# A gated recurrent and pooling layer: work tiles without zero columns in front, and all slots of 4,096 bytes

## The chip, the cores and the metric

The kernel runs on one core of one Trainium2 chip. The metric is the device time of one execution in microseconds. Engines are named as in the profile: PE is TensorE (matmuls), DVE is VectorE, ACT is ScalarE, POOL is GpSimd, SP is SyncE, which issues most DMAs.

## What is computed

One layer on x, 1,024 steps by 1,024 features, in float32 (reference, cut):

```python
h = x @ w_in + b_in                     # 1024 x 6144
xa, za, xb, zb, ga, gb = split(h)       # six of 1024
xa = causal_depthwise_conv(xa, conv_w, conv_b)          # 4 taps: y[t] = sum_k w[k] * x[t - 3 + k] + b
ya = rg_lru(xa, ...) * silu(za)         # gates by 64 x 64 head matrices, then h[t] = a[t] * h[t-1] + u[t]
yb = multiscale_pool(xb, ...) * silu(zb)
merged = sigmoid(ga) * (ya @ w_proj_a) + sigmoid(gb) * (yb @ w_proj_b)
x = layer_norm(alpha * x + merged @ w_out + b_out)

# the pool: feature group g of four has the window win = 2, 4, 8 or 16
cs = cumsum(xb, over time)
mean[t] = (cs[t] - cs[t - win]) / min(t + 1, win)
y = ((mean - xb) @ w_pool[g] + b_pool) * scale
```

So in front of the first step both the convolution and the window sums see zeros, and the first win - 1 columns of a pool are divided by their own count.

## The kernel before

Everything stands transposed: 128 features on the partitions and the 1,024 steps (S) along a row; H is 512, a half. Each product is done in float32r as three passes (high times high, high times low, low times high), and the 2 x 2 blocks of the large products are combined in seven products instead of eight. So most operands exist as a pair of tiles, high and low, made by a cast on ACT and a subtraction on DVE (`split`).

The first product is done group by group, 24 groups: G (two blocks of gates ga or gb), A (a block of xa and one of za) and B (a block of xb and one of zb), c being the block's number. While PE is at the next groups, DVE and ACT finish a group: for A the convolution (`a_front`), the head products `ps_g`, and the recurrence (`a_gates`); for B the window sums and the mean (`b_front`), then, for each pair of blocks, the product `ps_pool` with w_pool (`b_pool`). After the groups come the two merge products (tiles pa_, pc_, pe_) and the output product (oa, oc, oe) with the norm.

The program is first recorded as a list of tasks. A planner (`Plan.order`) then goes through them with costs of its own (`Plan.cost`) and due times, gives each engine its order, and emits everything from line 388; so the profile shows line 388 everywhere, and instructions are told apart by tile names. Each engine works through its own order strictly.

Tiles of 128 rows lie in pools: x (28 slots), w (10), r (4), k (10), e and g, in this order behind the constants. x, w and r slots have 4,096 bytes in each partition. A k slot is as large as the largest k tile. Which tiles are k tiles matters here: the front's working tiles xp, xc, xbp and the sums, xch and xcl (moving side of ps_g), mixh and mixl (moving side of ps_pool), and the pairs o1, o6, o7, o5, o3 and o4 (stationary side of oa and oc). The operands of the groups and of the merge products are x and w tiles throughout; the product oe has its operands in x and w tiles as well.

xp has three zero columns in front of the 1,024, xbp and the sums have PAD = 16, so that a shifted view reads zeros there. With 1,040 columns a k slot therefore takes 4,160 bytes. Where the slots start in a partition, as the built program lays them out (bytes):

| pool | before: first slot, step | start modulo 512 | after: first slot, step | start modulo 512 |
|---|---|---|---|---|
| x | 4,256, 4,096 | 160 | 4,320, 4,096 | 224 |
| w | 118,944, 4,096 | 160 | 119,008, 4,096 | 224 |
| r | 159,904, 4,096 | 160 | 159,968, 4,096 | 224 |
| k | 176,288, 4,160 | 160, 224, 288, 352, 416, 480, 32, 96, 160, 224 | 176,352, 4,096 | 224 |
| e | 217,888, 2,048 | 288 | 217,312, 2,048 | 224 |
| g | 226,080, 512 | 288 | 225,504, 512 | 224 |

Of the kernel before, what the change touches and what calls it, by code (L numbers as in the profile page):

```python
# [11 lines left out]
F32 = mybir.dt.float32  # L12
F32R = mybir.dt.float32r
AF = mybir.ActivationFunctionType
ALU = mybir.AluOpType

P = 128
S = 1024
D = 1024
NK = D // P  # L20
H = 512
# [4 lines left out]
PAD = 16  # L26
# [17 lines left out]
C_BIN = 0  # L44
C_CONVB = 48
C_CONVW = 56
# [354 lines left out]
def layer_kernel(ctx: ExitStack, tc: tile.TileContext, xq, x, w_in, par, wg, w_pool, wpa, wpb, w_out, rows, out):  # L401
    nc = Plan(tc)

    def pool(name, bufs, space=None):
        kw = {} if space is None else {"space": space}
        return Pool(ctx.enter_context(tc.tile_pool(name=name, bufs=bufs, **kw)), bufs, space is bass.MemoryType.DRAM)

    const = pool("const", 1)
# [3 lines left out]
    kpool = pool("kpool", NWORK)  # L412
# [11 lines left out]
    def rt(name, dt=F32, shape=(P, 2, H)):  # L424
        return rpool.tile(list(shape), dt, tag="r", name=name)

    def kt(name, dt=F32, w=S):
        return kpool.tile([P, w], dt, tag="k", name=name)

    def et(name):  # L430
        return epool.tile([P, H], F32, tag="e", name=name)
# [1 line left out]
    def bank(name):  # L433
        return psum.tile([P, H], F32, tag="ps", name=name)
# [5 lines left out]
    HALF = [slice(0, H), slice(H, S)]  # L440
    V, A = nc.vector, nc.scalar
# [4 lines left out]
    def pcol(base, c):  # L446
        return par_sb[:, base + c:base + c + 1]


    def split(raw, hi, lo):  # L450
        A.copy(hi, raw)
        V.tensor_tensor(lo, raw, hi.bitcast(F32), ALU.subtract)
# [141 lines left out]
    XA, ZA, XB, ZB, GA, GB = (8 * i for i in range(6))  # L594
# [13 lines left out]
    def weights_steps(i):  # L608
        kind, c = order[i]
        n1, n2 = blocks_of(kind, c)  # L610
        return Weights(f"{kind}{c}", w_in[n1], w_in[n2])
# [25 lines left out]
    def both(t, m1):  # L637
        for sl in HALF:
            V.tensor_tensor(t[:, sl], t[:, sl], m1, ALU.add)
# [83 lines left out]
    src = {}  # L723

    def a_outputs(c):
        xp, zt = kt(f"xp{c}", w=S + 3), kt(f"z{c}")
        V.memset(xp[:, 0:3], 0.0)

        def c11(ps, m1):
            V.scalar_tensor_tensor(xp[:, 3:3 + H], ps, pcol(C_BIN + XA, c), m1, ALU.add, ALU.add)  # L730

        def c12(ps, rest=None):
            if rest is None:
                A.activation(xp[:, 3 + H:], ps, AF.Identity, bias=pcol(C_BIN + XA, c))
            else:
                V.scalar_tensor_tensor(xp[:, 3 + H:], ps, pcol(C_BIN + XA, c), rest, ALU.add, ALU.add)

        def c21(ps, u2):
            V.tensor_tensor(zt[:, HALF[0]], ps, u2, ALU.add)

        def c22(ps, m7):
            V.tensor_tensor(zt[:, HALF[1]], ps, m7, ALU.add)

        def c2(m1):
            both(zt, m1)

        return (xp, zt), (c11, c12, c21, c22, c2)

    def a_front(c, xp, zt):
        xc = kt(f"xc{c}")  # L750
        V.tensor_scalar(xc, xp[:, 0:S], pcol(C_CONVW, 4 * c), pcol(C_CONVB, c), ALU.mult, ALU.add)
        for j in range(1, 4):
            V.scalar_tensor_tensor(xc, xp[:, j:j + S], pcol(C_CONVW, 4 * c + j), xc, ALU.mult, ALU.add)
        xh, xl = kt(f"xch{c}", F32R), kt(f"xcl{c}", F32R)
        split(xc, xh, xl)
        A.activation(zt, zt, AF.Silu, bias=pcol(C_BIN + ZA, c), scale=-1.0)
        return xc, xh, xl
# [80 lines left out]
        return finish, (c11, c12, c21, c22, c2)  # L838


    rcnt = const.tile([P, PAD], F32, name="rcnt")
    for t in range(PAD):
        nc.gpsimd.memset(rcnt[:, t:t + 1], 1.0 / (t + 1))
    mixed = [None] * NK
    szb = [None] * NK

    def b_outputs(c):
        xp, zt = kt(f"xbp{c}", w=S + PAD), kt(f"zb{c}")
        V.memset(xp[:, 0:PAD], 0.0)

        def c11(ps, m1):
            V.scalar_tensor_tensor(xp[:, PAD:PAD + H], ps, pcol(C_BIN + XB, c), m1, ALU.add, ALU.add)

        def c12(ps, rest=None):
            if rest is None:
                A.activation(xp[:, PAD + H:], ps, AF.Identity, bias=pcol(C_BIN + XB, c))
            else:
                V.scalar_tensor_tensor(xp[:, PAD + H:], ps, pcol(C_BIN + XB, c), rest, ALU.add, ALU.add)

        def c21(ps, u2):  # L860
            V.tensor_tensor(zt[:, HALF[0]], ps, u2, ALU.add)

        def c22(ps, m7):
            V.tensor_tensor(zt[:, HALF[1]], ps, m7, ALU.add)

        def c2(m1):
            both(zt, m1)

        return (xp, zt), (c11, c12, c21, c22, c2)

    def b_front(c, xp, zt):

        win = WINDOWS[c // 2]
        cur, step, lo = xp, 1, 0
        n = 0
        while step < win:
            nxt = kt(f"sum{n}_{c}", w=S + PAD)
            lo += step
            V.tensor_tensor(nxt[:, lo:], cur[:, lo:], cur[:, lo - step:S + PAD - step], ALU.add)
            cur, step, n = nxt, step * 2, n + 1  # L880
            yield
        m = cur[:, PAD:]
        e = win - 1
        V.tensor_tensor(m[:, 0:e], m[:, 0:e], rcnt[:, 0:e], ALU.mult)
        V.tensor_tensor(m[:, 0:e], m[:, 0:e], xp[:, PAD:PAD + e], ALU.subtract)
        V.scalar_tensor_tensor(m[:, e:], m[:, e:], 1.0 / win, xp[:, PAD + e:], ALU.mult, ALU.subtract)
        yield
        mh, ml = kt(f"mixh{c}", F32R), kt(f"mixl{c}", F32R)
        split(m, mh, ml)
        mixed[c] = (mh, ml)  # L890
        A.activation(zt, zt, AF.Silu, bias=pcol(C_BIN + ZB, c), scale=-1.0)
        szb[c] = zt
# [11 lines left out]
    def b_pool(g):  # L904
# [15 lines left out]
        if g == 1:  # L920
# [5 lines left out]
    sp, m, nl, y, z, z2, acc = (const.tile([P, 8], F32, name=n)  # L926
                                for n in ("sp", "sp_m", "sp_nl", "sp_y", "sp_z", "sp_z2", "sp_acc"))
# [23 lines left out]

    begin = ctx.enter_context(ExitStack())
    pass
    warm = kt("warm", F32R, H)
    V.memset(warm.bitcast(F32), 0.0)
    psw = bank("ps_warm")
    for i in range(WARM):
# [141 lines left out]
    w = weights_steps(1)  # L1099
# [19 lines left out]

    outs = g_outputs(GA, 0)[0]  # L1120
    tiles0, takes0 = a_outputs(0)
    g = Group("A0", w.out, X, *takes0)
    f5 = bank("f_A0")
# [23 lines left out]
    def first_rest(g=g):  # L1147
        g.m6()
        g.take(1, f5, g.u2)
        g.take(3, g.a, t5)  # L1150
        yield
        g.m4()
        yield
# [13 lines left out]
    for i in range(1, len(order)):  # L1167
        kind, c = order[i]
# [8 lines left out]
        if i == 1:  # L1177
            tiles = tiles0
        elif kind == "A":
            tiles, takes = a_outputs(c)  # L1180
        elif kind == "B":
            tiles, takes = b_outputs(c)
        else:
            finish, takes = g_outputs(GA if c < 4 else GB, c % 4)
# [20 lines left out]
        else:  # L1205
            g.m1()
            g.m2()
            if i == 2:
                rest = first_rest()
# [13 lines left out]
        if kind == "A":  # L1223
            def prev_end(c=c, tiles=tiles, i=i):
                front = a_front(c, *tiles)
                due.setdefault(i + 2, []).append(lambda: a_gates(c, *front, tiles[1]))
        elif kind == "B":
            def prev_end(c=c, tiles=tiles, i=i):
                for _ in b_front(c, *tiles):
                    pass  # L1230
                if c % 2 == 1:
                    pools.setdefault(i + 2, []).append(lambda: b_pool(c // 2))
        else:
            prev_end = finish
# [113 lines left out]
    def fronts():  # L1348
        for e in ends:
            yield from b_front(*e)  # L1350
# [6 lines left out]
    for i, (n, j) in enumerate(steps):  # L1357
# [7 lines left out]
        if j == 1:  # L1365
            a, c, m1, um = [[None] * KQ for _ in range(4)]
        X_, W_ = ([(hi_[:, k, :], lo_[:, k, :]) for hi_, lo_ in ops[i][o:o + 2] for k in range(2)] for o in (0, 2))
        for g in range(KQ):
# [4 lines left out]
            ps = a[g] if j in (1, 6, 5, 3) else c[g] if j != 2 else bank(f"pe_{n}{g}")  # L1373
# [31 lines left out]
            if (n, j, g) in CASTS:  # L1405
                k = CASTS.index((n, j, g))
# [12 lines left out]
    zt = {}  # L1419
# [76 lines left out]
    a, c = ([None] * KQ for _ in range(2))  # L1496
    operands(6)
    for i, j in enumerate(O_STEPS[:5]):
# [4 lines left out]
        for g in range(KQ):  # L1503
# [4 lines left out]
            ps = c[g] if j == 7 else a[g]  # L1508
# [13 lines left out]
    for g in range(KQ):  # L1522
# [3 lines left out]
        for sl in pieces:  # L1526
            ps = bank(f"oe_{g}_{sl.start}")[:, 0:sl.stop - sl.start]
# [58 lines left out]
```

## Time and profile before

| | |
|---|---|
| timed runs, us | 742.62, 743.99, 745.5; the median 743.99 |
| profiled execution | span 741.3 us from the first to the last instruction; the runs lie 1.3 to 4.2 us above it |
| mean granted TensorE clock | 0.998 |
| PE busy | 732.1 us, 99% |
| DVE busy | 599.6 us, 81% |
| ACT busy | 459.0 us, 62% |
| POOL busy | 68.2 us, 9% |
| traffic with main memory | 289 GB/s over the span |

The profile is one execution, with a page of sums and views of single stretches. In lists of instructions a row has the start, the length, the engine, the line, the operation, the tiles (out<-in, buffer numbers left out) and the shapes. A row of the chain that ended last has start, length, engine and output tile, with the number of instructions merged. A row of waits reads "who <- for whom: total, times, longest". A matmul's own length (389 ns) overlaps the next one's; how close they follow each other is seen from starts, or from a piece of the chain divided by its number of instructions.

### The profile page before, as it was taken

The numbers are of one execution on the slowest core, as the hardware profiler recorded it, in microseconds if no ns is written. First come the engines' busy times: TensorE is split into PE (matmuls) and PEld (weight loads), VectorE is DVE, ScalarE is ACT, GpSimd is POOL, SyncE is SP. The second block draws the span as 40 slices with busy tenths as digits, with TensorE's granted clock in tenths as the row PEclk, the third lists the DMA queues.
The fourth block names the chain that finished last, engine by engine and source line by source line (L and its number), as shares of the span: only waits on it lengthen the run. The fifth ranks groups of instructions, "written<-read, shape, count | busy, mean of one in ns | idle before, by whom it ended". The sixth has DMA issues, their size and how long they took to land.

```text
span 741.3 us, 8792 instructions
## 1 busy us (share of the span) xinstructions
PE 732.1 (99%) x3249; PEld 599.0 (81%) x3249; DVE 599.6 (81%) x749; ACT 459.0 (62%) x587; POOL 68.2 (9%) x118
## 2 busy tenths in 40 slices
PE   8999999999999999999999999999999999999996
PEld 6887887888788878888888888888888888888885
DVE  7999796959696878977986767879948886999676
ACT  7686959686877868688844445446543555324473
POOL 0071011111101111100011000100000000000021
PEclk9999999999999999999999999999999999999999
DMA  8237988588988989842187944998679996758657
GB/s 328 96 137 194 273 190 259 139 243 217 307 166 214 321 214 281 213 115 99 45 200 155 213 113 157 277 336 319 229 248 298 317 330 230 261 206 233 179 88 139
DMA packets 64227, 158.98 MB, mean 214 GB/s; under 512 B 4340, under 2 KB 8308, under 8 KB 64120
## 3 DMA queue, kind: packets, MB, share of 16 engines
q1 hardware_dynamic: 43512, 106.26, 41.3%
q0 software_dynamic: 20112, 51.91, 33.6%
q8 instruction: 25, 0.41, 0.2%
q10 hardware_dynamic: 560, 0.26, 0.1%
q14 instruction: 18, 0.15, 0.1%
HBM read 137.43 MB, written 77.07 MB: 289 GB/s over the span
## 4 chain that ended last, share of the span: by engine, by line
PE 98%; DMA 1%; DVE 1%; DVEq 0%; issue 0%
PE a_A L388 11%; PE a_B L388 11%; PE a_G L388 11%; PE oa L388 6%; PE pa_a L388 6%; PE pa_b L388 6%; PE c_B L388 6%; PE c_A L388 6%; PE c_G L388 5%; PE ps_pool L388 3%; PE oc L388 3%; PE pc_b L388 3%; PE pc_a L388 3%; PE e_B L388 3%; PE e_A L388 3%; PE ps_s L388 3%
## 5 line engine op out<-in xcount | busy, mean ns | idle before, releaser
L388 ACT ACT_TABLE_LOAD x38 | 48.8, 1283 | 3.0 <-issue 2.3
L388 DVE TENSOR_TENSOR i<-i,xc 128x1024 f32<-128x1024 f32 x8 | 9.8, 1224 | 26.6 <-ACT i L388 26.6
L388 DVE SCALAR_TENSOR_TENSOR xc<-xp,par_sb,xc 128x1024 f32<-128x1024 f32 x24 | 30.7, 1279 | 0.3
L388 PE MATMUL pa_a<-oh,oh 128*128 128x512 f32 x64 | 24.9, 389 | 0.0
L388 PE MATMUL pa_a<-oh,ol 128*128 128x512 f32 x64 | 24.9, 389 | 0.0
L388 PE MATMUL pa_b<-oh,oh 128*128 128x512 f32 x64 | 24.9, 389 | 0.0
L388 PE MATMUL pa_b<-ol,oh 128*128 128x512 f32 x64 | 24.9, 389 | 0.0
L388 PE MATMUL pa_b<-oh,ol 128*128 128x512 f32 x64 | 24.9, 389 | 0.0
L388 PE MATMUL pa_a<-ol,oh 128*128 128x512 f32 x64 | 24.9, 389 | 0.0
L388 ACT ACTIVATE zb<-zb,par_sb 128x1024 f32<-128x1024 f32 (+1 forms) x16 | 15.0, 939 | 13.7 <-DVE zb L388 13.6
L388 ACT ACTIVATE r<-ps_g,par_sb 64x512 f32<-64x512 f32 x32 | 21.9, 684 | 2.1 <-PE ps_g L388 1.2
L388 ACT ACTIVATE i<-ps_g,par_sb 64x512 f32<-64x512 f32 x32 | 21.9, 685 | 1.9 <-DVE r L388 1.4
L388 PE MATMUL c_A<-x64h,wd_A 128*128 128x512 f32 x64 | 21.0, 389 | 0.0
L388 PE MATMUL c_B<-x64h,wd_B 128*128 128x512 f32 x64 | 21.0, 389 | 0.0
L388 PE MATMUL ps_pool<-mixh,wp 128*128 128x512 f32 x64 | 20.6, 393 | 0.0
L388 POOL DMA_DIRECT2D out<-y x7 | 8.5, 1210 | 132.1 <-ACT sd L388 118.7
L388 PE MATMUL e_A<-x,wah_A 128*128 128x512 f32 x64 | 19.7, 389 | 0.0
L388 PE MATMUL e_B<-x,wah_B 128*128 128x512 f32 x64 | 19.7, 389 | 0.0
L388 POOL COPY paced<-pace 128x1 f32<-128x1 f32 x17 | 6.6, 387 | 128.7 <-ACT pace L388 128.7
L388 PE MATMUL c_G<-x64h,wd_G 128*128 128x512 f32 x56 | 18.4, 389 | 0.0
L388 DVE TENSOR_TENSOR_SCAN r<-a,i 128x1024 f32<-128x1024 f32 x8 | 18.3, 2282 | 0.1
L388 PE MATMUL e_G<-x,wah_G 128*128 128x512 f32 x56 | 17.2, 389 | 0.0
(521 smaller groups left out, 2535.9 us busy)
## 6 DMA issues: line engine op xcount, KB each, us to landing
sg<-sg SPq DMA_DIRECT2D x16, 512.0 KB, 3.6
ra_A<-in_w_in SPq DMA_DIRECT2D x8, 512.0 KB, 7.2
rb_A<-in_w_in SPq DMA_DIRECT2D x8, 512.0 KB, 7.8
xb<-bias SPq DMA_DIRECT2D x4, 1024.0 KB, 15.9
ya<-r SPq DMA_DIRECT2D x8, 512.0 KB, 6.3
xb<-in_x POOLq DMA_DIRECT2D x4, 1024.0 KB, 9.3
ra_B<-in_w_in SPq DMA_DIRECT2D x8, 512.0 KB, 4.8
rb_B<-in_w_in SPq DMA_DIRECT2D x8, 512.0 KB, 6.2
```

Source lines behind the costliest of these rows:

```text
L388: getattr(getattr(nc, t.op[0]), t.op[1])(*a, **k)
```

## The change

The zero columns in front go: xp, xbp and the sums are 1,024 columns wide, and with them every k slot has 4,096 bytes. The convolution starts from the newest tap, whose view is all of xp, and adds the older taps to the columns from j on. The window sums start at column `lo`, so the last of them gives the columns from win - 1 on; the first win - 1 columns come from a short scan over xbp with ones (a running sum), and are then multiplied with rcnt and so on as before. The two memsets for each pair of blocks go; a constant tile `ones` (64 bytes in each partition) comes, set by POOL. It lies among the constants and moves every pool behind them up by 64 bytes, the k slots' own shift apart (table above).

```diff
-    def kt(name, dt=F32, w=S):
-        return kpool.tile([P, w], dt, tag="k", name=name)
+    def kt(name, dt=F32):
+        return kpool.tile([P, S], dt, tag="k", name=name)
...
     def a_outputs(c):
-        xp, zt = kt(f"xp{c}", w=S + 3), kt(f"z{c}")
-        V.memset(xp[:, 0:3], 0.0)
+        xp, zt = kt(f"xp{c}"), kt(f"z{c}")
 
         def c11(ps, m1):
-            V.scalar_tensor_tensor(xp[:, 3:3 + H], ps, pcol(C_BIN + XA, c), m1, ALU.add, ALU.add)
+            V.scalar_tensor_tensor(xp[:, HALF[0]], ps, pcol(C_BIN + XA, c), m1, ALU.add, ALU.add)
...
     def a_front(c, xp, zt):
         xc = kt(f"xc{c}")
-        V.tensor_scalar(xc, xp[:, 0:S], pcol(C_CONVW, 4 * c), pcol(C_CONVB, c), ALU.mult, ALU.add)
+        V.tensor_scalar(xc, xp, pcol(C_CONVW, 4 * c + 3), pcol(C_CONVB, c), ALU.mult, ALU.add)
         for j in range(1, 4):
-            V.scalar_tensor_tensor(xc, xp[:, j:j + S], pcol(C_CONVW, 4 * c + j), xc, ALU.mult, ALU.add)
+            V.scalar_tensor_tensor(xc[:, j:], xp[:, :S - j], pcol(C_CONVW, 4 * c + 3 - j), xc[:, j:], ALU.mult, ALU.add)
...
-    rcnt = const.tile([P, PAD], F32, name="rcnt")
+    rcnt, ones = (const.tile([P, PAD], F32, name=n) for n in ("rcnt", "ones"))
+    nc.gpsimd.memset(ones, 1.0)
...
     def b_outputs(c):
-        xp, zt = kt(f"xbp{c}", w=S + PAD), kt(f"zb{c}")
-        V.memset(xp[:, 0:PAD], 0.0)
+        xp, zt = kt(f"xbp{c}"), kt(f"zb{c}")
...
         while step < win:
-            nxt = kt(f"sum{n}_{c}", w=S + PAD)
+            nxt = kt(f"sum{n}_{c}")
             lo += step
-            V.tensor_tensor(nxt[:, lo:], cur[:, lo:], cur[:, lo - step:S + PAD - step], ALU.add)
+            V.tensor_tensor(nxt[:, lo:], cur[:, lo:], cur[:, lo - step:S - step], ALU.add)
             cur, step, n = nxt, step * 2, n + 1
             yield
-        m = cur[:, PAD:]
+        m = cur
         e = win - 1
+        V.tensor_tensor_scan(m[:, 0:e], ones[:, 0:e], xp[:, 0:e], 0.0, ALU.mult, ALU.add)
         V.tensor_tensor(m[:, 0:e], m[:, 0:e], rcnt[:, 0:e], ALU.mult)
-        V.tensor_tensor(m[:, 0:e], m[:, 0:e], xp[:, PAD:PAD + e], ALU.subtract)
-        V.scalar_tensor_tensor(m[:, e:], m[:, e:], 1.0 / win, xp[:, PAD + e:], ALU.mult, ALU.subtract)
+        V.tensor_tensor(m[:, 0:e], m[:, 0:e], xp[:, 0:e], ALU.subtract)
+        V.scalar_tensor_tensor(m[:, e:], m[:, e:], 1.0 / win, xp[:, e:], ALU.mult, ALU.subtract)
```

PE's matmuls and their order stay as they are, and so does SP's order. On DVE the order changes at some places, because lengths and dependencies are others for the planner. The first place is DVE at the third pooled pair (blocks 4 and 5, window 8): sum_5 are block 5's window sums, mixl the low part of its mean, wcl_B the low part of a weight pair that PE takes in the group then running, zb the second half of the group's outputs. Before:

```order
L388 TENSOR_TENSOR sum_5_3825<-sum_5_3818 128x1037
L388 TENSOR_TENSOR wcl_B_3838<-sa_B_3796,wch_B_3828 128x1024
L388 TENSOR_TENSOR sum_5_3846<-sum_5_3825 128x1033
L388 TENSOR_TENSOR zb_3859<-c_B_3720,u_B_3789 128x512
L388 TENSOR_TENSOR zb_3859<-a_B_3768,m_B_3743 128x512
L388 SCALAR_TENSOR_TENSOR sum_5_3846<-sum_5_3846,xbp_3576 128x1017
L388 TENSOR_TENSOR sum_5_3846<-sum_5_3846,rcnt 128x7
L388 TENSOR_TENSOR sum_5_3846<-sum_5_3846,xbp_3576 128x7
L388 MEMSET xbp_3882 128x16
L388 TENSOR_TENSOR mixl_3891<-sum_5_3846,mixh_3880 128x1024
```

The same stretch of DVE in the changed kernel, from a little earlier on (a scan is printed as SCALAR_TENSOR_TENSOR, here with ones as its input):

```order
L388 SCALAR_TENSOR_TENSOR sum_5_3754<-ones,xbp_3580 128x7
L388 TENSOR_TENSOR sum_5_3754<-sum_5_3754,rcnt 128x7
L388 TENSOR_TENSOR sum_5_3754<-sum_5_3754,xbp_3580 128x7
L388 TENSOR_TENSOR mixl_3768<-sum_4_3707,mixh_3757 128x1024
...
L388 TENSOR_TENSOR sum_5_3820<-sum_5_3813 128x1021
L388 TENSOR_TENSOR zb_3833<-c_B_3716,u_B_3785 128x512
L388 TENSOR_TENSOR wcl_B_3837<-sa_B_3790,wch_B_3823 128x1024
L388 TENSOR_TENSOR zb_3833<-a_B_3763,m_B_3738 128x512
L388 TENSOR_TENSOR sum_5_3754<-sum_5_3820 128x1017
L388 SCALAR_TENSOR_TENSOR sum_5_3754<-sum_5_3754,xbp_3580 128x1017
L388 TENSOR_TENSOR mixl_3881<-sum_5_3754,mixh_3872 128x1024
```

The short operations on the first columns moved ahead of the previous block's mixl, since they need nothing but the first half of xbp; one zb sum moved in front of wcl_B.

The second place is DVE at the convolution of a block A (the second one). Before:

```order
L388 TENSOR_SCALAR xc_977<-xp_735,par_sb 128x1024
L388 SCALAR_TENSOR_TENSOR xc_977<-xp_735,par_sb,xc_977 128x1024
L388 TENSOR_TENSOR wbl_A_991<-rb_A_767,wbh_A_971 128x1024
L388 SCALAR_TENSOR_TENSOR xc_977<-xp_735,par_sb,xc_977 128x1024
L388 TENSOR_TENSOR sg_6_1007<-c_G_920,u_G_986 128x512
L388 SCALAR_TENSOR_TENSOR xc_977<-xp_735,par_sb,xc_977 128x1024
```

And in the changed kernel:

```order
L388 TENSOR_SCALAR xc_977<-xp_756,par_sb 128x1024
L388 SCALAR_TENSOR_TENSOR xc_977<-xp_756,par_sb,xc_977 128x1023
L388 TENSOR_TENSOR wbl_A_990<-rb_A_768,wbh_A_971 128x1024
L388 SCALAR_TENSOR_TENSOR xc_977<-xp_756,par_sb,xc_977 128x1022
L388 SCALAR_TENSOR_TENSOR xc_977<-xp_756,par_sb,xc_977 128x1021
L388 TENSOR_TENSOR sg_6_1011<-c_G_920,u_G_986 128x512
```

The last tap moved ahead of the sum for sg, and the taps are 1 to 3 columns shorter.

More of the change, by code (lines that the diff above doesn't have):

```diff
@@ L725, in a_outputs @@
     def a_outputs(c):
-        xp, zt = kt(f"xp{c}", w=S + 3), kt(f"z{c}")
-        V.memset(xp[:, 0:3], 0.0)
+        xp, zt = kt(f"xp{c}"), kt(f"z{c}")
         def c11(ps, m1):
-            V.scalar_tensor_tensor(xp[:, 3:3 + H], ps, pcol(C_BIN + XA, c), m1, ALU.add, ALU.add)
+            V.scalar_tensor_tensor(xp[:, HALF[0]], ps, pcol(C_BIN + XA, c), m1, ALU.add, ALU.add)
         def c12(ps, rest=None):
             if rest is None:
-                A.activation(xp[:, 3 + H:], ps, AF.Identity, bias=pcol(C_BIN + XA, c))
+                A.activation(xp[:, HALF[1]], ps, AF.Identity, bias=pcol(C_BIN + XA, c))
             else:
-                V.scalar_tensor_tensor(xp[:, 3 + H:], ps, pcol(C_BIN + XA, c), rest, ALU.add, ALU.add)
+                V.scalar_tensor_tensor(xp[:, HALF[1]], ps, pcol(C_BIN + XA, c), rest, ALU.add, ALU.add)
         def c21(ps, u2):
@@ L847, in b_outputs @@
     def b_outputs(c):
-        xp, zt = kt(f"xbp{c}", w=S + PAD), kt(f"zb{c}")
-        V.memset(xp[:, 0:PAD], 0.0)
+        xp, zt = kt(f"xbp{c}"), kt(f"zb{c}")
         def c11(ps, m1):
-            V.scalar_tensor_tensor(xp[:, PAD:PAD + H], ps, pcol(C_BIN + XB, c), m1, ALU.add, ALU.add)
+            V.scalar_tensor_tensor(xp[:, HALF[0]], ps, pcol(C_BIN + XB, c), m1, ALU.add, ALU.add)
         def c12(ps, rest=None):
             if rest is None:
-                A.activation(xp[:, PAD + H:], ps, AF.Identity, bias=pcol(C_BIN + XB, c))
+                A.activation(xp[:, HALF[1]], ps, AF.Identity, bias=pcol(C_BIN + XB, c))
             else:
-                V.scalar_tensor_tensor(xp[:, PAD + H:], ps, pcol(C_BIN + XB, c), rest, ALU.add, ALU.add)
+                V.scalar_tensor_tensor(xp[:, HALF[1]], ps, pcol(C_BIN + XB, c), rest, ALU.add, ALU.add)
         def c21(ps, u2):
@@ L953, in layer_kernel @@
     pass
-    warm = kt("warm", F32R, H)
+    warm = kt("warm", F32R)[:, :H]
     V.memset(warm.bitcast(F32), 0.0)
```

## Prediction

> **What bounds the kernel now.** I read the page first, then the list of who waits for whom, filtered to TensorE, then the chain that ended last in order of time, and at the end the timeline at the places where TensorE takes something that VectorE has only just finished.
>
> ```profile
> span 741.3 us, 8792 instructions
> PE 732.1 (99%) x3249; PEld 599.0 (81%) x3249; DVE 599.6 (81%) x749; ACT 459.0 (62%) x587; POOL 68.2 (9%) x118
> PEclk9999999999999999999999999999999999999999
> PE 98%; DMA 1%; DVE 1%; DVEq 0%; issue 0%
> ...
> PE ps_warm L388 <- DVE xp L388: 1.4, 1, 1.4
> PE ps_s L388 <- DVE xb L388: 0.3, 1, 0.3
> ```
>
> TensorE is 98% of the chain, its granted clock is full in all slices, and it waits for another engine twice, 1.7 us in all, both in the first 10 us. VectorE, on which nearly the whole edit lies, is busy 81% of the span and holds nothing up. So the edit can bring time in one way only: by making matmuls start closer together. It can cost time in two ways: by making them start further apart, or by making VectorE late where TensorE now just finds its operand ready.
>
> The chain shows how closely the matmuls follow each other. Its pieces, each with start, length and number of instructions:
>
> ```profile
> 400.00 5.57 PE ps_pool L388 x24
> ...
> 424.64 5.44 PE a_B L388 x24
> ...
> 443.68 5.55 PE ps_pool L388 x24
> ...
> 473.75 5.56 PE ps_pool L388 x24
> ...
> 541.91 5.54 PE ps_pool L388 x24
> ...
> 580.14 10.88 PE pa_b L388 x48
> ...
> 634.54 10.88 PE pc_b L388 x48
> ...
> 656.30 22.21 PE oa L388 x96
> 678.51 11.19 PE oc L388 x48
> 689.70 22.19 PE oa L388 x96
> 711.89 2.77 PE oc L388 x12
> ...
> 717.39 2.75 PE oc L388 x12
> ...
> 722.87 2.75 PE oc L388 x12
> ...
> 728.36 2.76 PE oc L388 x12
> 731.12 2.87 PE oe L388 x24
> ```
>
> A 512-column matmul takes 10.88 / 48 = 226.7 ns in a_, pa_ and pc_, whose operands are both from x and w tiles. In ps_pool it takes 5.57 / 24 = 232 ns, in oa 22.21 / 96 = 231.4 ns. There is no wait in these pieces, and form and clock are the same. What sets them apart is where an operand lies: ps_pool's moving side is mixh and mixl, and the stationary side of oa and oc is o1 to o7, all k tiles. Only k tiles have slots of 4,160 bytes. Every x and w tile starts 160 bytes past a multiple of 512; I call this its phase. The ten k slots have eight phases, 64 bytes apart. Within a tile the operands step by 512 or 2,048 bytes, which keeps the phase, and pa_b and pc_b step through whole tiles without a trace of it. So I read the extra 4.6 to 5 ns as the price of operands that change phase against each other.
>
> **The change, part by part.**
>
> *Slots of 4,096 bytes.* Every x, w, r, k, e and g tile now starts at one phase, 224. If the price belongs to unequal phases, ps_pool, oa and oc fall to 226.7 ns. From the pieces above:
> - ps_pool: 5.57 + 5.55 + 5.56 + 5.54 = 22.22 us, against 4 x 5.44 = 21.76: 0.46 us.
> - oa: 22.21 + 22.19 = 44.40, against 4 x 10.88 = 43.52: 0.88 us.
> - oc: 11.19 against 10.88, and 2.77 + 2.75 + 2.75 + 2.76 = 11.03 against 10.88: 0.46 us.
>
> Together 1.80 us, all of it on the chain. The head pairs ps_g also read k tiles. The chain shows what they and the matmuls behind them take:
>
> ```profile
> 72.60 1.58 PE ps_g L388 x12
> 74.19 3.00 PE a_G L388 x12
> ...
> 112.55 1.60 PE ps_g L388 x12
> 114.15 2.99 PE a_G L388 x12
> ```
>
> Twelve half-height matmuls run as six pairs, and 6 x 226.7 ns would be 1.36 us; a_G behind them has 0.28 us over 2.72. If all of this 0.5 us were phase, eight chunks would give 4 us; if none, nothing. Slots and phases differ from chunk to chunk, yet the two chunks agree within 0.02 us, so I put it down to the change of the tile's height and take nothing; within the 0.02 us that they differ, eight chunks could give 0.2 us either way.
>
> *VectorE's work.* Rows for its prices:
>
> ```profile
> L388 DVE MEMSET xp<- x8: 61/61/61, 1.3 to 274.6; 128x3 f32 x8
> L388 DVE TENSOR_TENSOR sum<-xbp x8: 1230/1233/1244, 361.7 to 505.3; 128x1039 f32<-128x1039 f32 x8
> L388 DVE TENSOR_TENSOR sum<-sum,rcnt x8: 149/156/166, 373.3 to 527.3; 128x1 f32<-128x1 f32 x2, 128x3 f32<-128x3 f32 x2, 128x7 f32<-128x7 f32 x2, 128x15 f32<-128x15 f32 x2
> L388 DVE SCALAR_TENSOR_TENSOR xc<-xp,par_sb,xc 128x1024 f32<-128x1024 f32 x24 | 30.7, 1279 | 0.3
> L388 DVE TENSOR_TENSOR_SCAN r<-a,i 128x1024 f32<-128x1024 f32 x8 | 18.3, 2282 | 0.1
> L388 DVE SCALAR_TENSOR_TENSOR a<-a,r 128x1024 f32<-128x1024 f32 x8 | 9.8, 1224 | 4.6 <-ACT r L388 4.6
> ```
>
> Sixteen memsets go: 16 x 0.06 = 1.0 us. The 20 window sums lose 16 of some 1,039 elements each: 20 x 16 x 1.19 ns = 0.4 us. Eight short scans come. None is in the trace: 0.06 us (the memset) and 2.28 us (the long scan) are the ends; a length of 1 to 15 is nearest the 0.156 us of the rcnt row, so 8 x 0.2 = 1.6 us. The 24 taps are 1 to 3 elements shorter, and the operand that starts off the slot's beginning is now xc, read and written, instead of xp. They may land at the 1.224 us of the row whose operands are all level (1.3 us less) or pay the present 55 ns twice (1.3 us more); I take no change. In all VectorE gets 0.2 us more. The ends are 0.5 - 1.0 - 0.4 - 1.3 = 2.2 us less and, with the long scan's price, 18.2 - 1.0 - 0.4 + 1.3 = 18 us more, in an engine with 142 us idle. None of it is on the chain while its results come in time.
>
> *In time?* The two places after the start where TensorE comes closest to waiting for something whose surroundings on VectorE the edit reorders, both at the third pooled pair (timeline, start and length in us, and TensorE's first use):
>
> ```profile
> 465.39 1.24 DVE L388 TENSOR_TENSOR sum<-sum 128x1037 f32<-128x1037 f32 x1
> 466.55 1.22 DVE L388 TENSOR_TENSOR wcl_B<-sa_B,wch_B 128x1024 fp32r<-128x1024 f32 x1
> 468.83 0.68 DVE L388 TENSOR_TENSOR zb<-c_B,u_B 128x512 f32<-128x512 f32 x1
> 472.68 1.23 DVE L388 TENSOR_TENSOR mixl<-sum,mixh 128x1024 fp32r<-128x1024 f32 x1 [1.14 <-ACT mixh L388]
> 468.61 0.39 PE L388 MATMUL a_B<-x64h,wcl_B 128*128 128x512 f32 x1
> 474.51 0.39 PE L388 MATMUL ps_pool<-mixl,wp 128*128 128x512 f32 x1
> ```
>
> mixl ends at 473.91, 0.60 us before its use. Its three short operations (one more than before) now stand ahead of the previous chunk's mixl, so its own chain gets some 0.3 us shorter (two operations of about 0.156 us that stood in it). wcl_B ends at 467.77, 0.84 us before its use, and now has a zb sum ahead of it, which holds VectorE some 0.6 us: 0.2 us are left. So no wait comes in, by a small margin; if it were missed by as much as one further zb sum, TensorE would stand for 0.5 us.
>
> *Nothing on the path:* POOL's one more memset (ones) lies at the start of a queue that is busy 9%, and its first user comes after 370 us. No DMA is added or moved on SP's queue. The head of the program ends with the first loads and their casts, which stay.
>
> Sum: 741.3 - 1.8 = 739.5 us of span. The runs lie 1.3 to 4.2 us above the profiled span, the median 2.7; so 743.99 - 1.8 = 742.2 us. Half a per cent (3.7 us) is about what a measurement of this kernel can tell from no change, so this counts as the same.
>
> **Rivals.**
>
> *The spacing stays: 744.0.* Then the 231 ns come from something else, for instance from the upper part of the memory in which all k tiles lie. For it: all ten slots are there. Against it: a fixed handicap would give one fixed interval, and ps_pool, oa and oc, which mix slots differently, give piece means of 229 (2.75 / 12) to 233 ns (11.19 / 48). The Trainium skill, "TensorE: Matmul & The Clock Gate", section "Wait — 56ns, not 53.3ns?", gives a warm matmul 512 columns at 2.4 GHz plus a fixed 2.5 ns, 215.7 ns wherever its operands lie. By that rule the spacing would not move, but its figure is 11 ns under the 226.7 ns here, and in the trace the addition is not fixed.
>
> *Contention instead of phase: 744.0 as well.* TensorE could be slowed in these stages by other engines' reads. Against it: pa_b, at 226.7 ns, runs beside as much traffic. The skill's page "SBUF — State Buffer", section "Who interferes with whom", says that TensorE waits for no other engine there; the trace agrees in pa_b and cannot tell for oa.
>
> *The new phase is a bad one: 757, the slow side.* All tiles move from phase 160 to 224. If a place has its price and not a difference of places, and 224 costs what the k tiles cost on average, then the 3,249 - 288 - 96 - 96 = 2,769 matmuls outside oa, oc, ps_pool and ps_g go from 226.7 to 231.4 ns: 2,769 x 4.7 ns = 13 us more. It decides for slower from 3.7 / 2,769 = 1.3 ns each on. For it: no run here has all tiles at 224. Against it: x and w tiles alone give 226.7 in every stage, which fits a rule of differences, and by such a rule any common phase is as good as another.
>
> *The new phase is a better one: under 740.3.* It needs (3.7 - 1.8) / 3,249 = 0.6 ns more from each matmul. Same arguments, turned round; the ps_g bound (4 us) alone would also do it, 738.
>
> **How the numbers follow.** Forecast 742.2 with VectorE in time or up to 1 us late: 0.70. Spacing unchanged, for either reason: 0.16, 744. New phase worse: 0.06. Better, or ps_g falls: 0.08. Faster by over 0.5% is the last, 0.08; slower the third, 0.06; the same 0.86. Timed runs of one kernel here scatter 2.9 us, a median of them perhaps 1. The range takes in the forecast and the unchanged spacing with that: 740.3 to 745.2.
>
> **What would show it.** Right: the chain's pieces ps_pool x24 at 5.44, oa x96 at 21.76 and oc x48 at 10.88 us, with pa_b and a_B as now; no new line where TensorE waits; sum<-ones scans of 0.15 to 0.25 us; VectorE within 4 us of 599.6. Wrong: pa_b x48 away from 10.88 (phase 224 has a price of its own), oa still at 22.2 (not phase), or TensorE waiting for wcl_B or mixl near 468 to 474 us.

## The result, and the profile after

| | before | after |
|---|---|---|
| timed runs side by side, median (lowest to highest) | 742.79 us (742.59 to 745.5), 7 runs | 740.62 us (739.65 to 741.03), 7 runs |
| ratio after to before | | 0.9967, 95% interval 0.9955 to 0.9978 |
| profiled execution, span | 741.3 us | 738.3 us |

The changed kernel is 2.2 us faster by the medians, and 2.5 us by the ratio (742.79 x 0.0033; 1.6 to 3.3 by the interval). That is a real gain, and it stays under the half per cent that was set as a mark, so it counts as the same. Forecast were 742.2 us, measured 740.62. Of the 1.6 us between them, 1.2 lie in the starting point: the three runs shown at first had the median 743.99, all seven have 742.79.

The page's first lines of the changed kernel (span, and busy time of each engine with its number of instructions), and the waits of TensorE:

```profile
span 738.3 us, 8785 instructions
PE 729.5 (99%) x3249; PEld 599.4 (81%) x3249; DVE 600.8 (81%) x741; ACT 459.0 (62%) x587; POOL 67.9 (9%) x119
...
PE ps_warm L388 <- DVE warm L388: 1.4, 1, 1.4
```

PE has as many matmuls as before and 2.6 us less busy time; DVE has eight instructions fewer and 1.2 us more busy time; there is no new line in the list of waits. So the time came out of the spacing of the matmuls. The chain shows where (start, length, engine and tile, number of matmuls):

```profile
28.13 2.72 PE a_A L388 x12
...
71.65 1.59 PE ps_g L388 x12
73.24 2.94 PE a_G L388 x12
...
398.93 5.44 PE ps_pool L388 x24
...
442.45 5.44 PE ps_pool L388 x24
...
472.39 5.44 PE ps_pool L388 x24
...
540.39 5.44 PE ps_pool L388 x24
...
578.47 10.88 PE pa_b L388 x48
...
654.63 21.76 PE oa L388 x96
676.39 10.88 PE oc L388 x48
687.27 21.76 PE oa L388 x96
```

All four ps_pool pieces, both oa pieces and oc now have 226.7 ns for each matmul, as pa_b always had. Those are the pieces that stood at 5.54 to 5.57, 22.2 and 11.19 us.

The span fell by 3.0 us, and it splits at the start of the first group. Before, the chain read there:

```profile
29.08 2.72 PE a_A L388 x12
```

The head ended at 29.08 us and now ends at 28.13: 0.95 us. The rest took 741.3 - 29.08 = 712.2 us and now takes 738.3 - 28.13 = 710.2. The difference, 2.1 us from unrounded ends, is the 1.80 us of ps_pool, oa and oc and some 0.3 us in small pieces: 0.16 in the four pieces behind the ps_pool (5.48, 2.76, 2.76 and 10.92 us before, 5.44, 2.72, 2.72 and 10.88 now) and 0.10 in the eight behind the ps_g (3.00, 2.99 and then 2.94 to 2.96 before, 2.94 or 2.95 now). The head is told apart from the change in the next section: its end moves from kernel to kernel by more than a microsecond without a rule.

### The profile page after: what moved, and what is told of

The parts are those of the page before. It is cut to its first block, busy times and chain, and to the rows that moved or that the text cites. A ratio compares the mean times of both kernels' runs of the same rounds, so it can differ in the third digit from the quotient of the medians.

```text
span 738.3 us, 8785 instructions
## 1 busy us (share of the span) xinstructions
PE 729.5 (99%) x3249; PEld 599.4 (81%) x3249; DVE 600.8 (81%) x741; ACT 459.0 (62%) x587; POOL 67.9 (9%) x119
## 4 chain that ended last, share of the span: by engine, by line
PE 99%; DVE 1%; DVEq 0%; issue 0%
PE a_A L388 11%; PE a_B L388 11%; PE a_G L388 11%; PE oa L388 6%; PE pa_a L388 6%; PE pa_b L388 6%; PE c_B L388 6%; PE c_A L388 6%; PE c_G L388 5%; PE ps_s L388 3%; PE oc L388 3%; PE pc_b L388 3%; PE pc_a L388 3%; PE ps_pool L388 3%; PE e_B L388 3%; PE e_A L388 3%
## 5 line engine op out<-in xcount | busy, mean ns | idle before, releaser
L388 DVE SCALAR_TENSOR_TENSOR xc<-xp,par_sb,xc 128x1023 f32<-128x1023 f32 (+2 forms) x24 | 30.7, 1281 | 0.5
```

The source lines that it names most:

```text
L388: getattr(getattr(nc, t.op[0]), t.op[1])(*a, **k)
```

## The experiments

"The rest" below is the span less the start of the first a_A, so the head's scatter is out of it. All kernels are the changed kernel with one edit.

**k4160: all of the change but the level slots.** The k slots get their 4,160 bytes back; the views without zero columns, the scans and the missing memsets stay, and so does the order on every engine.

```diff
-        return kpool.tile([P, S], dt, tag="k", name=name)
+        return kpool.tile([P, S + 16], dt, tag="k", name=name)[:, :S]
```

> The changed kernel with one thing undone: each k slot has 4,160 bytes again, so the ten k slots have eight phases, while x, w and r tiles keep phase 224. Arithmetic and the order on every engine are those of the changed kernel. Theory (operands of unequal phase follow each other more slowly): the chain's pieces ps_pool x24 go back to about 5.55 us, oa x96 to 22.2 and oc x48 to 11.2, and the span is about 1.8 us longer than the changed kernel's 738.3. Rival (the removed columns and memsets brought it, or the upper part of the memory costs): pieces stay at 5.44, 21.76 and 10.88. The 1 us by which the head of the program was shorter in the changed kernel's profile: if it comes from the k slots, ps_s ends near 29.0 us again; if from the memsets or from chance, it need not.

Measured: 742.91 us (11 runs) against 742.24 of the kernel before (19 runs), ratio 1.0005 (0.9996 to 1.0014). phase0 below, timed on the same occasion with level slots, has 740.46. The chain of k4160:

```profile
398.56 5.57 PE ps_pool L388 x24
...
578.63 10.88 PE pa_b L388 x48
654.79 22.23 PE oa L388 x96
677.01 11.18 PE oc L388 x48
```

The old spacing is back in the same three products, and the rest takes 712.4 us, as before the change (712.2). So the whole gain is the slots' step; what VectorE does in another way is worth nothing that can be measured. The head ended at 27.67 us here, earlier than in either kernel, with the old slots: the 0.95 us are not the slots' doing.

**w4160: the same handicap on other operands.** Now the w slots, which hold one operand of every group, are 4,160 bytes apart.

```diff
-        return wpool.tile(list(shape), dt, tag="w", name=name)
+        t = wpool.tile([P, S + 16], dt, tag="w", name=name)[:, :S]
+        return t if len(shape) == 2 else t.rearrange("p (i s) -> p i s", i=2)
```

> The changed kernel with the w slots instead of the k slots at 4,160 bytes: ten w slots with eight phases, x at 224, r and k at 352. Nearly all matmuls of the groups (a_, c_, e_, b_, f_) take their stationary side from w tiles. Theory: each of them goes from 226.7 to about 231 ns, 1,700 to 1,800 of them, so 8 us more in the groups; oa and oc have their moving side there (w tiles against k at 352) and go to about 231 as well, 1.3 us; ps_pool 0.4 us; pa_ and pc_ (x tiles on both sides) stay at 10.88 a piece. Span about 748. Rival (a place high in the memory costs, or only k tiles do): groups stay at 2.72 a piece, span 738.

Measured: 751.0 us (4 runs), ratio 1.0117 (1.01 to 1.0133); the rest 720.3 us. The chain:

```profile
347.66 5.57 PE a_B L388 x24
...
587.60 10.88 PE pa_b L388 x48
...
663.77 22.24 PE oa L388 x96
```

The groups go to 231 ns on average (single pieces 226.7 to 233.3), pa_b (both operands in x slots, like those of all merge products and of oe, by the addresses in the built program) stays at 226.7, and oa, with one side in w and the other in k, is slow again though the k slots are level. It is not the k pool and not its place in the memory: it goes by where the two sides lie.

**gap64: one constant difference.** In the kernel before and in w4160 the difference between the sides also changes from tile to tile. Here 64 unused bytes between the x pool and all later pools make it constant: each w tile starts 64 bytes later, modulo 512, than each x tile.

```diff
     xpool = pool("xpool", 28)
+    gap = pool("gap", 1)
...
+    gap_sb = gap.tile([P, 16], F32, name="gap_sb")
+    nc.gpsimd.memset(gap_sb, 0.0)
```

> The changed kernel with 64 unused bytes between the x pool and the pools behind it: x tiles at phase 224, all w, r, k, e and g tiles at 288. Now the two sides of a group's matmul differ by a constant 64 bytes, while each side by itself keeps its phase from matmul to matmul. Theory A (a matmul pays when a side's phase differs from that side's phase in the matmul before): pieces of the groups stay at 2.72, span 738. Theory B (it pays for the difference between its two sides): every group piece moves off 2.72 by the same amount, in either direction; ps_pool and oa, whose sides are both behind the gap, stay at 5.44 and 21.76.

Measured: 753.96 us (one run), the rest 723.1 us, 12.9 more than the changed kernel. The chain:

```profile
351.34 5.60 PE a_B L388 x24
...
410.14 5.46 PE ps_pool L388 x24
...
592.21 10.88 PE pa_b L388 x48
...
701.05 21.76 PE oa L388 x96
```

Every piece of a group has 5.60 / 24 = 233.3 ns, the same throughout, and ps_pool, oa and pa_b, with both sides on one side of the gap, have the old 226.7 or are close to it (ps_pool 227.5 to 228.3). Within a group nothing changes here from one matmul to the next, and the price is there in full. So the theory that only a change costs has fallen; what costs is a standing difference between the moving and the stationary side. A change costs a little besides: where ps_pool or oa follows a product whose moving side lies in front of the gap, the first five to ten spacings lie between 224 and 236 ns before they settle at 226.7, which makes 0.02 to 0.04 us each time.

One thing stays open. The load of a matmul's stationary side (PEld) begins in this trace some 3 ns after the matmul ahead of it has started, so it runs beside that one's moving side. In the groups the stationary sides are all w tiles, the next matmul's as well. So the runs don't say whether a matmul's own stationary side counts or the one that is loaded meanwhile.

**phase0: all tiles at another common place.** 288 unused bytes among the constants move all pools from 224 to a multiple of 512.

```diff
+    gap_sb = const.tile([P, 72], F32, name="gap_sb")
+    nc.gpsimd.memset(gap_sb, 0.0)
```

> The changed kernel with 288 unused bytes among the constants: all x, w, r, k, e and g tiles at phase 0 instead of 224. Theory (differences of phase count, not a place): every piece as in the changed kernel, 2.72 us for 12 matmuls, span 738 to 739. Rival (a common phase has its own price): all pieces move, 1 ns each would give 3 us.

Measured: 740.46 us (8 runs), ratio 0.9973 (0.9962 to 0.9983); the rest 710.1 us, as in the changed kernel (710.2). The chain:

```profile
342.19 5.44 PE a_B L388 x24
...
655.02 21.76 PE oa L388 x96
```

A common start of 224 is as good as 0, and the x and w tiles of the kernel before had the same 226.7 ns at 160: none of the three has a price of its own.

**gap32, gap128, gap256, gap448 and gap480: how the price goes with the difference.** The edit is that of gap64 with another number of bytes, one run each.

> As gap64 with 32 unused bytes: w, r, k, e and g tiles 32 bytes behind the x tiles' phase. gap64 gave 233.3 ns in every group piece, 6.7 ns (16 columns of 4 bytes at 2.4 GHz) over the changed kernel. Theory 'columns' (the next matmul waits for as many columns as the sides are apart): 8 columns, 226.7 + 3.3 = 230.0 ns. Theory 'lines' (only whole 64-byte steps count): 226.7. A time under 226.7 would mean a spacing that beats the changed kernel.

> 128 bytes between the sides. The few places in w4160 where three matmuls in a row had this difference had about 232 ns (228 to 241). Theory 'columns without end': 32 columns, 240.0 ns. Theory 'period of 128 bytes': 226.7. Theory 'period of 256 bytes' (w4160 had like values at 64 and 320, at 128 and 384, at 192 and 448): about 232 to 233.

> 256 bytes between the sides. Theory 'period of 256 bytes': 226.7 again in all group pieces, span as the changed kernel's, 738. 'Columns without end': 253 ns. 'Period of 512 bytes': anything between, w4160 had 226 to 233 in 44 places.

> 448 bytes, which is 64 bytes short of the period of 512: the w side stands 64 bytes before the x side. w4160 had 225 to 232 ns in 52 such places, 229 on average. If the sign counts (the stationary side ahead of the moving side gives time instead of costing it), down to 220.0 ns and a span of 726; if the sign does not count, 233.3 as gap64; from w4160's places, about 229.

> 480 unused bytes between the sides: by the period of 256 bytes that gap256 showed, the w side stands 32 bytes before the x side. Known by now: 0 and 256 bytes 226.7 ns, 32 and 64 bytes 233.3, 128 bytes 232.7, 448 bytes 228.9. If the extra falls off towards the end of the period, 227 to 229 ns and a span of 739 to 743; if one 32-byte step to this side gives time, under 226.7 and a span under 738.

A piece of a_B in the chains of gap32, gap128, gap256, gap448 and gap480, in this order:

```profile
351.48 5.60 PE a_B L388 x24
```

```profile
351.09 5.57 PE a_B L388 x24
```

```profile
342.64 5.44 PE a_B L388 x24
```

```profile
345.53 5.49 PE a_B L388 x24
```

```profile
350.89 5.60 PE a_B L388 x24
```

| bytes between the sides | 0 | 32 | 64 | 128 | 256 | 448 | 480 |
|---|---|---|---|---|---|---|---|
| a group's matmul, ns | 226.7 | 233.3 | 233.3 | 232.7 | 226.7 | 228.9 | 233.3 |
| the rest of the span, us | 710.2 | 723.2 | 723.1 | 721.8 | 710.1 | 714.7 | 723.2 |
| timed, us | 740.62 | 754.18 | 753.96 | 753.29 | 740.87 | 745.5 | 753.63 |

A difference of 256 bytes is free, so it isn't 512 that counts, as in the tables above. The trace of w4160 tells more, since its differences vary and each matmul's addresses are known from the built program. Where the difference stayed the same over four matmuls in a row, the mean spacings are:

| difference in w4160, bytes | 0 and 256 | 64 and 320 | 128 and 384 | 192 and 448 |
|---|---|---|---|---|
| mean spacing, ns | 226.7 and 227.1 | 233.3 and 233.5 | 232.1 and 232.9 | 228.9 and 228.9 |

Differences that are 256 bytes apart cost the same (9 to 57 spacings each, 865 at 0), and they agree with the constant gaps: the period is 256 bytes. 32 bytes cost as much as 64, so the price is no measure of the distance. 448 (64 short of the next multiple) costs a third of what 64 costs, and 480 (32 short) costs all of it: neither a rule of distance nor one of sign gives both. No difference gave less than 226.7 ns. At 128 the pieces vary a little, between 5.56 and 5.60 us for 24.

**longscan: is VectorE's work really off the path?** Eight scans of 1,024 columns come on top, into the window sum's tile just before the last sum overwrites it.

```diff
             nxt = kt(f"sum{n}_{c}")
             lo += step
+            if 2 * step == win:
+                V.tensor_tensor_scan(nxt, xp, xp, 0.0, ALU.mult, ALU.add)
```

> The changed kernel with eight scans of all 1,024 columns more, one for each block B, 2.28 us each by the row of the recurrence's scan: VectorE busy about 619 us instead of 600.8. Their results are overwritten by the window sums, so nothing else changes. Theory (VectorE's work is off the path; it costs only where a result comes late): matmul spacing 226.7 everywhere; TensorE waits at most at the third pooled pair, where mixl has 0.6 us to spare and one scan of 2.28 us can stand in front: up to 2 us there, so 0 to 4 us in all. Rival (the removed and added VectorE operations count in full): 18 us longer, 756.

Measured: 744.58 us (7 runs, 743.06 to 746.97), ratio 1.0023 (1.001 to 1.0037). First lines of the page, and TensorE's instructions at the third pooled pair (in brackets the idle time ahead and what ended it):

```profile
PE 733.1 (98%) x3249; PEld 600.6 (81%) x3249; DVE 618.3 (83%) x749; ACT 459.3 (62%) x587; POOL 69.8 (9%) x119
PEclk9999999999999999999999999899999999999999
```

```profile
473.95 0.50 PE L388 MATMUL ps_pool<-mixl,wp 128*128 128x512 f32 x1 [0.75 <-DVE mixl L388]
...
475.76 0.50 PE L388 MATMUL ps_pool<-mixh,wp 128*128 128x512 f32 x1 [1.09 <-ACT mixh L388]
477.02 0.80 PE L388 MATMUL ps_pool<-mixl,wp 128*128 128x512 f32 x1 [0.76 <-DVE mixl L388]
477.61 1.06 PE L388 MATMUL ps_pool<-mixh,wp 128*128 128x512 f32 x2
478.47 0.63 PE L388 MATMUL ps_pool<-mixl,wp 128*128 128x512 f32 x1
478.89 1.06 PE L388 MATMUL ps_pool<-mixh,wp 128*128 128x512 f32 x2
```

```profile
477.02 7.74 PE ps_pool L388 x20
```

VectorE is busy 618.3 - 600.8 = 17.5 us longer, and the time rises by 4.0 us against the changed kernel's median (744.58 - 740.62, taken on another occasion; the kernel before had 742.79 there and 742.61 here). That is far from the 18 us of the rival. The work is free until a mixl comes late, at the place the prediction had named. There TensorE waits 2.6 us in three pieces, and then its clock is halved: the three matmuls from 477.61 to 478.89 take 1.28 us, 427 ns each, and 20 matmuls take 7.74 us where 20 x 226.7 ns are 4.53. So 3.2 us of what this profiled execution lost (746.97 us, the slowest of the seven) come from the clock and not from the waits. The expectation had the place right. The waits came to 2.6 us instead of up to 2, and the clock was not in it: "matmul spacing 226.7 everywhere" failed there.

## Why the prediction was right or wrong

**Right: the 1.80 us.** ps_pool, oa and oc fell to 5.44, 21.76 and 10.88 us, term by term as worked out; k4160 gave them back, with the rest of the change in place.

**Right for a partly wrong reason: "the price of operands that change phase against each other".** The groups at 226.7 and the k products at 231 to 233 ns fitted both a price for a change from matmul to matmul and one for a standing difference, since in the kernel before the k products have both. The text took the first wording and rested on a "rule of differences" for its forecast; gap64 shows that the standing difference makes up most of it. Both give the same for this change, so the number didn't suffer; that the forecast did not hang on the wording was luck. Nor is it 512 bytes that count: 256 is enough. With the table's price for each matmul's own difference in the kernel before (0, 64, 128 or 192 bytes modulo 256, with 448 taken for 192), ps_pool would have 231.0 ns, oa 230.6 and oc 229.9 on average; measured were 231.5, 231.3 and 231.5. The 0.5 to 1.6 ns that are missing would fit the small price of changes, but no run shows that by itself. What in the chip makes it so is open.

**Mis-sized: VectorE "0.2 us more"; it was 1.2** (599.6 to 600.8 us). The lengths of the instructions came out near the forecast. The scans had 1.3 us in all instead of 1.6 (row: lowest, median, highest in ns), the first window sums were 15 ns shorter each (1233 to 1218), near the 0.4 us taken for the 20 of them, and the taps were 2 ns longer on average.

```profile
L388 DVE TENSOR_TENSOR_SCAN sum<-ones,xbp x8: 150/158/189, 372.2 to 518.4; 128x1 f32<-128x1 f32 x2, 128x3 f32<-128x3 f32 x2, 128x7 f32<-128x7 f32 x2, 128x15 f32<-128x15 f32 x2
```

What failed is the step from lengths to busy time. An instruction here begins before the one ahead of it has ended, and busy time counts such a stretch once. The short operations of the first pooled pair, before:

```profile
372.12 1.22 DVE L388 TENSOR_TENSOR wal_B<-ra_B,wah_B 128x1024 fp32r<-128x1024 f32 x1
373.25 0.15 DVE L388 TENSOR_TENSOR sum<-sum,rcnt 128x1 f32<-128x1 f32 x1
373.44 0.16 DVE L388 TENSOR_TENSOR sum<-sum,xbp 128x1 f32<-128x1 f32 x1
373.55 0.07 DVE L388 MEMSET xbp<- 128x16 f32 x1
```

And in the changed kernel:

```profile
371.04 1.22 DVE L388 TENSOR_TENSOR wal_B<-ra_B,wah_B 128x1024 fp32r<-128x1024 f32 x1
372.17 0.15 DVE L388 TENSOR_TENSOR_SCAN sum<-ones,xbp 128x1 f32<-128x1 f32 x1
372.36 0.16 DVE L388 TENSOR_TENSOR sum<-sum,rcnt 128x1 f32<-128x1 f32 x1
```

The memset ends 0.02 us behind its neighbour (373.62 against 373.60), so it adds 0.02 us and not 0.07. The product with rcnt used to start 0.09 us before wal_B's end (373.34); now the scan has that place, and the product stands free behind it. All starts and lengths of both traces, with each stretch counted for the instruction that reaches it first, give this: the sixteen memsets held 0.2 us and not "1.0" (three lay wholly inside a neighbour, thirteen stuck out by 10 to 25 ns), the scans hold 0.7, the products with rcnt 0.7 more than before, the taps, which follow their neighbours in another order, 0.5 more, the window sums 0.3 less, and everything else 0.2 less. An instruction's length is neither what its removal frees nor what its addition costs, where it overlaps its neighbour. It made no difference to the time, since VectorE was not the bound.

**Right with two steps wrong: the margins at the third pooled pair.** VectorE, then TensorE's load of wcl_B and its first matmuls with wcl_B and mixl, then ACT, in the changed kernel:

```profile
465.74 1.21 DVE L388 TENSOR_TENSOR wcl_B<-sa_B,wch_B 128x1024 fp32r<-128x1024 f32 x1
...
471.32 1.22 DVE L388 TENSOR_TENSOR mixl<-sum,mixh 128x1024 fp32r<-128x1024 f32 x1 [1.39 <-ACT mixh L388]
```

```profile
467.00 0.19 PEld L388 LDWEIGHTS a_B<-x64h,wcl_B 128*128 128x128 f32 x1
```

```profile
467.23 0.39 PE L388 MATMUL a_B<-x64h,wcl_B 128*128 128x512 f32 x1
...
473.14 0.39 PE L388 MATMUL ps_pool<-mixl,wp 128*128 128x512 f32 x1
```

```profile
469.75 0.59 ACT L388 COPY u_B<-a_B 128x512 f32<-128x512 f32 x1 [2.20 <-PE a_B L388]
470.24 1.05 ACT L388 CAST mixh<-sum 128x1024 fp32r<-128x1024 f32 x1
```

The first step is wcl_B. It is a stationary side, so its first use is the load at 467.00 and not the matmul at 467.23, from which the prediction counted. Before, that load began at 468.38: wcl_B, done at 467.77, had 0.61 us to spare and not 0.84, and the zb sum of some 0.6 us ahead of it used that up. So "0.2 us are left" is wrong. wcl_B now ends at 466.95 and the load follows 0.05 us later, as in k4160, phase0 and gap256. In these four, four to six spacings from there on are wider, up to 236 ns, and the piece of the chain takes 2.74 or 2.75 us; before, and in longscan, where 0.31 us are left, all stay at 226 or 227 ns and the kernel before has 2.72 for the piece. So TensorE just felt it, by some 0.02 us, too little for the list of waits. That it was no more was luck: nothing was left of the margin.

The second step is mixl. It ends at 472.54 and is used at 473.14: still 0.60 us, not 0.9. "Its own chain gets some 0.3 us shorter" failed, because the chain does not run through VectorE alone: the cast mixh on ACT stands behind the copy u_B, which waits for TensorE's a_B. What VectorE saved ahead of mixh became a longer wait for mixh, 1.39 us instead of 1.14. longscan shows how thin the 0.60 us are.

**The ps_g term, taken as 0 +/- 0.2 out of 4.** It was the small one: ps_g itself stayed at 1.57 to 1.60 us, and the pieces behind it gave 0.10 us in all. The two chunks that the prediction compared, with 3.00 and 2.99 us, were the two highest of the eight; the others stood at 2.94 to 2.96 already. All eight now have 2.94 or 2.95 with level operands, so the rest of the extra time of ps_g isn't phase. The 0.16 us behind the ps_pool pieces were in no term.

**Not foreseen: the head.** "The head of the program ends with the first loads and their casts, which stay." They stay, but when they land does not: the last load in the chain of the head, an xr, landed at 8.88 us before, 5.07 in k4160 and 7.49 in phase0, and in the changed kernel the chain has none. The first a_A started at 29.08 us before, 28.13 after, 27.67 in k4160, 28.51 in phase0 and 28.96 in gap256. A span of one profiled execution carries this spread of 1.4 us, which is why the difference of the spans (3.0) is larger than that of the runs (2.2 to 2.5) and than the rest's (2.1).

**The rivals.** "The spacing stays" and contention fell with the first look at ps_pool and oa, and k4160 and w4160 turn the effect on and off with nothing but addresses. The rule of the Trainium skill named there ("TensorE: Matmul & The Clock Gate", section "Wait — 56ns, not 53.3ns?": a fixed addition of 2.5 ns) differs from all rows here (float32r): the addition to 213.3 ns was 13.4 ns with level sides and 20.0 ns with a gap of 64 bytes, so it is not fixed. "The new phase is a bad one" and "a better one" fell with pa_b and the groups, which stayed at 226.7 ns at 224, and with phase0.

## What to carry to other kernels

Where TensorE is the bound, divide the pieces of its chain by their number of matmuls and compare products of one shape: if one kind is some 2 to 3% slower without a wait, compare where its two operands start, and make all slots a multiple of 256 bytes behind a common start. Read a saving from the stage that bounds; here 17.5 us of further work on VectorE cost 4 us, and what the edit changed there brought nothing. Before the time of a removed instruction is booked as gained, look how much of it lay inside its neighbour's. And count the margin of a stationary operand to the load of the weights (PEld), which came 0.23 us before the matmul here.

## What was unexpected of the hardware

- **A matmul's spacing goes by the difference of its two operands' starts, modulo 256 bytes** (float32r, 512 columns): 226.7 ns at 0 and 256, 233.3 at 32, 64 and 480, 232.7 at 128, 228.9 at 448. In this kernel a pool misplaced by 32 bytes costs 13 us, 1.8%, with no wait in the profile that would tell of it.
- **Half the clock after scattered waits.** In longscan TensorE started five matmuls between 472.81 and 477.02 us, no wait among them longer than 1.1 us, and afterwards ran at 427 ns a matmul for some 6 us (granted clock 0.50 between 476.5 and 483.2 us). The Trainium skill, "TensorE: Matmul & The Clock Gate", Part 1, names an idle window of about 3.4 us as what halves the clock; here the engine wasn't wholly idle over such a stretch: by the lengths of its matmuls it was busy for 1.4 of the 3.4 us before the clock fell. Of the seven timed runs, those with a mean granted clock of 0.994 or 0.995 took 744.4 to 747.0 us and the two with 0.998 took 743.1 and 743.4: the scatter goes with the clock.
- **A short operation can be nearly free.** The sixteen memsets of 61 or 72 ns held 0.2 us of VectorE's busy time, a fifth of their lengths, and the eight short scans hold 0.7 of their 1.3 us; the rest lies inside the time of the instructions ahead.
